# One transformer layer in split single precision: operands loaded in place, last sums moved into gate and up, last projections reordered, memory laid out anew

## The chip, the cores and the metric

One core of a Trainium2 chip runs the kernel. The metric is device microseconds from start to end, as the median of several runs. Engines are named as in the profile: PE is TensorE, DVE VectorE, ACT ScalarE, POOL GpSimd; SP is SyncE, whose queue issues nearly all DMA transfers here. Lines are written L91, and they are lines of the kernel before unless said otherwise.

## The reference

One layer over a sequence of 2048 positions of width 1024, in float32: a mixing half (band attention beside a gMLP) and a SwiGLU feed-forward half, each with a norm ahead and a residual behind.

```python
h = rmsnorm(x, mix_norm_g)
q, k, v, u, vg = split(h @ w_in)                  # 1024 -> 2560
a = band_attention(q, k, v, ...)                  # 8 heads of 64, chunks of 64, 8 chunks back
g = spatial_gating(u, vg, ...)                    # blocks of 128 positions, 8 groups
mix = concat(rmsnorm(a, att_out_norm_g), rmsnorm(g, gmlp_out_norm_g))
x = x + mix @ w_out                               # 1024 -> 1024
h = rmsnorm(x, ffn_norm_g)
gate, up = split(h @ w_ffn_in)                    # 1024 -> 2 * 2816
x = x + (silu(gate) * up) @ w_ffn_out             # 2816 -> 1024
```

## The kernel before

**Precision.** Every large product is three matmuls. `split` (L86) makes of a float32 operand a rounded part (a cast on ACT) and the rest (a subtraction on DVE); `mm3` (L90) adds high by high, high by low and low by high into one PSUM bank. A 128x512 matmul of this kind begins every 0.2267 us.

**Stages.** 1: input projection, gMLP, early attention heads, up to about 530 us. 2: the late heads (tiles 4 to 15 of 128 positions), and between their scores, `flip` and `values` pieces of the output projection, up to 916 us. 3: gate and up. 4: the down-projection. Stages 1 and 2 write PE's order by hand (`manual_schedule`); all other orders are set by a scheduler at build time, which works with a model of the machine.

**Stage 2.** `out_piece(m, n, kt)` (L584) is one `mm3` for tile m, half n of the 1024 columns and one of eight 128-row blocks; kt 0 to 3 are the gMLP half of the input (woh4 to woh7), 4 to 7 the attention half. `mix_g` and `mix_a` (L139, L142) transpose a half of the mixed input on PE and split it into mh and ml. At kt = 7, DVE adds the bank to xm, ACT squares and sums, POOL makes the factor (L81, L83), DVE writes the normalised tile h2 (L599). `operands(m)` (L603) then makes eight transposes of it on PE, copies them into hT on ACT and stores them to y_d. `add_fill` writes the list of pieces, and `feed` takes from it.

**What y_d is.** Gate and up are made with seven products of half size in place of eight (a Strassen form): of a tile t of the first four in its half of the sequence and tile t + 4 come the seven moving operands y_d[hf][o], four of which are sums, made by four 128x512 subtractions on POOL (L620 to L623) as soon as tile t + 4 is there. hf is the half of the sequence (tiles 0 to 7, 8 to 15).

**Stage 3.** For each hf and each p = 0 to 10 (256 columns of 2816) there are 14 products: o = 0 to 6, and s = 0 for gate, 1 for up. A product is 12 matmuls (`product`, L770). Weights: `w_raw` loads wir, `w_sums` makes s3, s1 (in wir) and s2 on POOL, `w_op` splits one operand into wih and wil; `generate` runs five products ahead. `prep(hf)` loads the seven moving operands into three buffers (gt3, which also hold the results g) as ynat, four DMAs of 256 KB each with pieces of 512 bytes, and splits each into yh and yl in two halves. `use` and `emit` bring the banks into g; at the end of each p, g and c go to f_d. For hf = 1 the seven operands are loaded and split again while PE goes on.

**Stage 4.** `product` (L871) runs seven products of 22 halves each: ar from f_d, split into ah and al, and a weight, split into oh and ol. The weights of the first product (w11, called w_0, w_2 ... in the order) are kept, the first two in the pool wk40.

**Memory.** Pools are laid out by hand at the left or right end of the memory, and a tile that lies where another was waits for the last reader or writer of that one. Before the change the first wih buffers and the weight sums (wi3, sum3) share addresses with mx2, that holds hT and the sums t of the last tile; wk40 and part of wt4 in stage 4 share with gt3.

## Time and profile before

| | |
|---|---|
| median of 3 runs | 2232.69 us (2232.06 to 2233.97) |
| profiled execution | 2236.06 us |
| its span, first to last instruction | 2234.3 us |
| mean granted clock of PE | 0.988 |
| PE busy | 2160.9 us (97%), 12090 matmuls |
| DVE busy | 1295.2 us (58%) |
| ACT busy | 901.9 us (40%) |
| POOL busy | 920.1 us (41%) |
| DMA | 356.60 MB, mean 160 GB/s |

A profile of one execution gives for each engine its instructions with start and length, and for idle time what released the engine at its end. PE's time in the span is nearly all busy, so what is left to win is in a few gaps; they are found in the list of waits and then read in the timeline of the place. A busy time of one matmul is longer than the distance between two, because they overlap.

### The profile page before, as it was taken

The numbers are of one execution on the slowest core, as the hardware profiler recorded it, in microseconds if no ns is written. First come the engines' busy times: TensorE is split into PE (matmuls) and PEld (weight loads), VectorE is DVE, ScalarE is ACT, GpSimd is POOL, SyncE is SP. The second block draws the span as 40 slices with busy tenths as digits, with TensorE's granted clock in tenths as the row PEclk, the third lists the DMA queues.
The fourth block names the chain that finished last, engine by engine and source line by source line (L and its number), as shares of the span: only waits on it lengthen the run. The fifth ranks groups of instructions, "written<-read, shape, count | busy, mean of one in ns | idle before, by whom it ended". The sixth has DMA issues, their size and how long they took to land.

```text
span 2234.3 us, 32028 instructions
## 1 busy us (share of the span) xinstructions
PE 2160.9 (97%) x12090; PEld 1797.2 (80%) x12090; DVE 1295.2 (58%) x1809; ACT 901.9 (40%) x1639; POOL 920.1 (41%) x792
## 2 busy tenths in 40 slices
PE   8999999999999999599999999999999979999999
PEld 7888887887888888478888887788888858888787
DVE  4367335774677666566565668666566524545554
ACT  6434444543555555433333334333333323222322
POOL 1253114330002101556666665767666512613444
PEclk9999999999999999799999999999999989999999
DMA  7243615648878875822322327232323343733473
GB/s 257 80 132 117 222 57 170 167 145 259 286 225 278 269 237 170 269 90 90 122 91 104 108 94 229 93 123 90 123 90 121 138 150 128 278 136 110 156 240 139
DMA packets 183802, 356.60 MB, mean 160 GB/s; under 512 B 15328, under 2 KB 68576, under 8 KB 182112
## 3 DMA queue, kind: packets, MB, share of 16 engines
q1 hardware_dynamic: 183504, 354.55, 48.1%
q8 instruction: 95, 1.56, 0.3%
q14 instruction: 59, 0.48, 0.1%
q10 hardware_dynamic: 144, 0.00, 0.0%
HBM read 253.83 MB, written 100.66 MB: 159 GB/s over the span
## 4 chain that ended last, share of the span: by engine, by line
PE 53%; DMA 2%; DVE 2%; SPq 1%; issue 1%; POOL 1%; ACT 0%; DVEq 0%; ACTq 0%; POOLq 0%
PE bank L91 18%; PE bank L93 18%; PE bank L92 18%; DMA ynat<-y_d 1%; DVE yl L88 1%; SPq L723 0%; DMA y_d<-t 0%; DVE wil L88 0%; DMA w<-in_w_fo 0%; SPq L845 0%; DMA b<-y_d 0%; POOL t L621 0%; DVE xo L894 0%; POOL wir L742 0%; DMA wir<-in_w_fi 0%
## 5 line engine op out<-in xcount | busy, mean ns | idle before, releaser
L91 PE MATMUL bank<-yh,wih 128*128 128x512 f32 x1232 | 481.6, 391 | 17.2 <-ACT wih L87 17.2
L93 PE MATMUL bank<-yh,wil 128*128 128x512 f32 x1232 | 480.9, 391 | 4.4 <-DVE wil L88 4.1
L92 PE MATMUL bank<-yl,wih 128*128 128x512 f32 x1232 | 481.0, 390 | 0.0
L91 PEld LDWEIGHTS bank<-yh,wih 128*128 128x128 f32 x1232 | 232.3, 189 | 66.1 <-ACT wih L87 18.1
L93 PEld LDWEIGHTS bank<-yh,wil 128*128 128x128 f32 x1232 | 231.9, 188 | 55.4 <-DVE wil L88 7.3
L92 PEld LDWEIGHTS bank<-yl,wih 128*128 128x128 f32 x1232 | 232.4, 189 | 48.6
L91 PE MATMUL ps<-wh,xh 128*128 128x512 f32 x640 | 252.4, 399 | 7.9 <-ACT wh L87 7.9
L91 PE MATMUL bank<-oh,ah 128*128 128x512 f32 x616 | 239.9, 392 | 15.4 <-ACT oh L87 15.4
L92 PE MATMUL ps<-wl,xh 128*128 128x512 f32 x640 | 251.4, 394 | 2.5 <-DVE wl L88 2.5
L93 PE MATMUL ps<-wh,xl 128*128 128x512 f32 x640 | 251.2, 393 | 0.0
L92 PE MATMUL bank<-ol,ah 128*128 128x512 f32 x616 | 239.6, 389 | 0.0
L88 DVE TENSOR_TENSOR al<-ar,ah 128x1024 fp32r<-128x1024 f32 x77 | 107.8, 1400 | 211.4 <-ACT ah L87 211.4
L93 PE MATMUL bank<-oh,al 128*128 128x512 f32 x616 | 220.8, 389 | 2.1 <-DVE al L88 2.1
L88 DVE TENSOR_TENSOR wil<-s,wih 128x512 fp32r<-128x512 f32 x132 | 134.0, 1017 | 122.6 <-ACT wih L87 122.6
L87 ACT CAST wih<-s 128x512 fp32r<-128x512 f32 x132 | 81.9, 622 | 303.6 <-POOL s L743 158.3
L88 DVE TENSOR_TENSOR wil<-wir,wih 128x512 fp32r<-128x512 f32 x176 | 195.4, 1111 | 6.3 <-ACT wih L87 6.3
L87 ACT CAST ah<-ar 128x1024 fp32r<-128x1024 f32 x77 | 81.2, 1055 | 284.5 <-PE bank L92 266.5
L87 ACT CAST wih<-wir 128x512 fp32r<-128x512 f32 x176 | 108.9, 621 | 188.3 <-PE bank L92 178.0
L781 POOL TENSOR_TENSOR g<-up,g 128x512 f32<-128x512 f32 x88 | 122.8, 1395 | 108.9 <-DVE up L780 80.6
L91 PEld LDWEIGHTS bank<-oh,ah 128*128 128x128 f32 x616 | 116.6, 190 | 40.3 <-ACT oh L87 15.8
L91 PEld LDWEIGHTS ps<-wh,xh 128*128 128x128 f32 x640 | 121.2, 190 | 31.2 <-ACT wh L87 7.9
L92 PEld LDWEIGHTS ps<-wl,xh 128*128 128x128 f32 x640 | 121.1, 189 | 26.7 <-DVE wl L88 3.5
(182 smaller groups left out, 4051.3 us busy)
## 6 DMA issues: line engine op xcount, KB each, us to landing
wir<-in_w_fi SPq DMA_DIRECT2D x88, 512.0 KB, 4.4
ar<-f_d SPq DMA_DIRECT2D x77, 512.0 KB, 3.3
kTw<-kT_d SPq DMA_DIRECT2D x96, 320.0 KB, 4.2
f_d<-g SPq DMA_DIRECT2D x22, 1024.0 KB, 4.0
wr<-in_w_in SPq DMA_DIRECT2D x40, 512.0 KB, 5.0
f_d<-c SPq DMA_DIRECT2D x22, 768.0 KB, 6.1
wor<-in_w_fo SPq DMA_DIRECT2D x66, 256.0 KB, 3.5
ynat<-y_d SPq DMA_DIRECT2D x56, 256.0 KB, 5.1
```

Of the source, the lines that this page charges most:

```text
L87: nc.scalar.copy(hi, src)
L88: nc.vector.tensor_sub(lo, src, hi.bitcast(F32))
L91: nc.tensor.matmul(ps, lhsT=lh, rhs=rh, start=first, stop=False)
L92: nc.tensor.matmul(ps, lhsT=lh, rhs=rl, start=False, stop=False)
L93: nc.tensor.matmul(ps, lhsT=ll, rhs=rh, start=False, stop=last)
L781: nc.gpsimd.tensor_tensor(g[:, i], t, g[:, i], op=ALU.mult)
```

## The change

Four things are changed together.

*In place.* `prep` has no buffers of its own. Each operand is loaded into the memory of its yl, as float32; ACT casts it into yh and DVE subtracts in place. There are two DMAs of 512 KB for an operand, with pieces of 4 KB, and yh and yl keep the order (tile, block k, column), so that a product's moving operand, `y[:, :, k]`, is four blocks of 128 columns. y_d is one tensor for the four tiles of an operand.

*The last tiles' sums.* For tiles 13, 14, 15 `operands` stores the two halves of hT alone. `combine(n)`, n = 0 to 5, makes the sums for 256 columns: four loads, four subtractions on POOL, four stores. They are written in the loops p = 2 to 7 of hf = 0; the scheduler puts them into p = 0 to 2.

*The last projections.* `add_tail` writes the pieces of tiles 14 and 15: tile 14's gMLP half for both n, tile 15's, `operands(13)`, tile 14's attention half, tile 15's, with `operands(14)` in it. Both banks of these tiles are one tile of pS.

*Memory.* The projection weights are four pools instead of one, and stage 3's pools lie so that wi3, sum3, wr3 and y0 are over the attention's buffers, y1 and y2 over woh4 to woh7, y3 and y4 over woh0 to woh3, y5 and y6 over mixed inputs and h2. gt3 has two buffers. wk40 and wt4 of stage 4 are now over wi3 and wr3.

The diff, cut:

```diff
-    y_d = [[[dram.tile([P, 512], F32, name=f"y_d{i}_{o}_{j}") for j in range(4)] for o in range(7)] for i in range(2)]
+    y_d = [[dram.tile([P, 4, 512], F32, name=f"y_d{i}_{o}") for o in range(7)] for i in range(2)]
+    h_d = {m: dram.tile([P, 512], F32, name=f"h_d{m}") for m in range(NT - 3, NT)}
...
-        for n, bufs in (("pr", 3), ("pp", 2), ("an", 2), ("sa", 4), ("vt", 6), ("bt", 1), ("qd", 2), ("kw", 5)):
+        for n, bufs in (("pr", 3), ("pp", 2), ("sa", 4), ("vt", 6), ("bt", 1), ("qd", 2), ("kw", 5), ("an", 2)):
...
-        wo2, mx["T"] = pool(stack, "wo2", 1), pool(stack, "mxT", 2)
         for kt in (4, 5, 6, 7, 0, 1, 2, 3):
+            if kt % 2 == 0:
+                wo2 = pool(stack, f"wo2{kt}", 1)
...
+        mx["T"] = pool(stack, "mxT", 2)
...
-        hp = pool(st_out, "h2", 1)
-        mx["2"], sm = pool(st_att, "mx2", 2, "right"), pool(st_att, "sm2", 4, "right")
+        mx["2"], hp, sm = pool(st_att, "mx2", 2, "right"), pool(st_att, "h2", 1, "right"), pool(st_att, "sm2", 4, "right")
...
-                po[m, n] = pS.tile([P, 2, 512], F32, tag="S", name="po")[:, 0] if flush and n else pO.tile([P, 512], F32, tag="po", name="po")
+                if m < NT - 2:
+                    po[m, n] = pO.tile([P, 512], F32, tag="po", name="po")
+                elif n == 0:
+                    both = pS.tile([P, 2, 512], F32, tag="S", name="po2")
+                    po[m, 0], po[m, 1] = both[:, 0], both[:, 1]
...
-            y = [y_d[hf][o][t % 4] for o in range(7)]
-            if t < 4:
+            y = [y_d[hf][o][:, t % 4] for o in range(7)]
+            if m in h_d:
+                nc.sync.dma_start(h_d[m], hT[:, :512])
+                nc.sync.dma_start(y[5], hT[:, 512:])
+            elif t < 4:
...
-            if m == NT - 1:
-                fill.extend(("piece", piece(n, kt)) for kt in range(KT) for n in range(2))
-                fill.insert(len(fill) - 4, ("operands", m - 1))
-                return
...
-                    if kt == 3 and m > 0:
+                    if kt == 3 and m > 0 and (n == 0 or m < NT - 3):
                         fill.append(("a" if n else "g", m + 1))
+
+        def add_tail():
+            def half(m, kts):
+                fill.extend(("piece", lambda n=n, kt=kt: out_piece(m, n, kt)) for n in range(2) for kt in kts)
+
+            m = NT - 1
+            half(m - 1, range(4))
+            fill.extend((("a", m - 1), ("g", m)))
+            half(m, range(4))
+            fill.append(("operands", m - 2))
+            half(m - 1, range(4, 8))
+            fill.append(("a", m))
+            half(m, range(4, 8))
+            fill.insert(len(fill) - 3, ("operands", m - 1))
...
-        for m in range(NT):
+        for m in range(NT - 2):
             add_fill(m)
...
+                if i == len(LATE):
+                    add_tail()
...
-        yp = {0: pool(st, "y0", 1, "right")}
-        gt, wr, wi, sp3 = (pool(st, n, b, "right") for n, b in (("gt3", 3), ("wr3", 1), ("wi3", 6), ("sum3", 1)))
-        for i in (1, 2):
-            yp[i] = pool(st, f"y{i}", 1)
+        y0, wr, wi, sp3, gt = (pool(st, n, b, "right") for n, b in (("y0", 1), ("wr3", 1), ("wi3", 6), ("sum3", 1), ("gt3", 2)))
+        yp = [y0] + [pool(st, f"y{i}", 1) for i in range(1, 6)]
         tm = pool(st, "tm3", 1)
-        for i in (3, 4, 5, 6):
-            yp[i] = pool(st, f"y{i}", 1, "left" if i < 5 else "right")
-        cb = pool(st, "cb3", 1, "right")
+        yp.append(pool(st, "y6", 1))
+        cb, df = pool(st, "cb3", 1), pool(st, "df3", 1)
...
-                yh = yp[o].tile([P, 4, 512], F32R, tag="yh", name=f"yh{hf}{o}")
-                yl = yp[o].tile([P, 4, 512], F32R, tag="yl", name=f"yl{hf}{o}")
+                yh = yp[o].tile([P, 4, 4, P], F32R, tag="yh", name=f"yh{hf}{o}")
+                yl = yp[o].tile([P, 4, 4, P], F32R, tag="yl", name=f"yl{hf}{o}")
                 ys.append((yh, yl))
-                r = gt.tile([P, 4, 512], F32, tag="g", name="ynat")
-                for i in range(4):
-                    nc.sync.dma_start(r[:, :, i * P : (i + 1) * P], y_d[hf][o][i].rearrange("p (k t) -> p k t", k=4))
-                for k in range(0, 4, 2):
-                    split(yh[:, k : k + 2], yl[:, k : k + 2], r[:, k : k + 2])
+                for i in (slice(0, 2), slice(2, 4)):
+                    r = yl[:, i].bitcast(F32)
+                    nc.sync.dma_start(r, y_d[hf][o][:, i].rearrange("p i (k t) -> p i k t", k=4))
+                    split(yh[:, i], yl[:, i], r)
             return ys
+
+
+        def combine(n):
+            m, c = NT - 3 + n // 2, slice(n % 2 * 256, n % 2 * 256 + 256)
+            y = [y_d[1][o][:, m % 4, c] for o in range(7)]
+            h1, h2, b1, b2, t1, t2, t3, t4 = (df.tile([P, 256], F32, tag=t, name=t) for t in ("dh1", "dh2", "db1", "db2", "dt1", "dt2", "dt3", "dt4"))
+            for dst, src in ((h1, h_d[m][:, c]), (h2, y[5]), (b1, y[0]), (b2, y[4])):
+                nc.sync.dma_start(dst, src)
+            nc.gpsimd.tensor_sub(t1, h1, b1)
+            nc.gpsimd.tensor_sub(t2, h2, t1)
+            nc.gpsimd.tensor_sub(t3, h2, h1)
+            nc.gpsimd.tensor_sub(t4, b2, t2)
+            for o, src in ((1, t2), (2, t1), (3, t3), (6, t4)):
+                nc.sync.dma_start(y[o], src)
...
+            bk = bk.rearrange("p (i t) -> p i t", i=4)
             for k in range(4):
-                mm3(bk, w[0][:, k], w[1][:, k], y[0][:, k], y[1][:, k], k == 0, k == 3)
+                mm3(bk, w[0][:, k], w[1][:, k], y[0][:, :, k], y[1][:, :, k], k == 0, k == 3)
...
+            if hf == 0 and 2 <= p < 8 and (o, s) == (1, 0):
+                combine(p - 2)
```

In the orders below, rows are instructions of one engine in sequence; the line numbers of the second fence of a pair are those of the kernel after (L92 to L94 is `mm3`, L613 the transposes of `operands`, L739 the loads of `prep`, L749 and L755 the loads and stores of `combine`, L762 `w_raw`).

PE at the end of stage 2 and the start of stage 3, before: the last piece of tile 15 (po), the transposes of tile 15 (pth), the first product (bank).

```order
L91 MATMUL po<-woh_5184,mh_11363 128x512
L92 MATMUL po<-wol_5185,mh_11363 128x512
L93 MATMUL po<-woh_5184,ml_11364 128x512
L608 MATMUL pth<-ident,h_11546 128x128 x8
L91 MATMUL bank<-yh_11678,wih 128x512
L92 MATMUL bank<-yl_11679,wih 128x512
```

After: the same last piece, then the first product (yh_11610 is operand o = 0), and in product o = 2 (yh_11626) the transposes of tile 15.

```order
L92 MATMUL po_11354<-woh_5151,mh_11345 128x512
L93 MATMUL po_11354<-wol_5152,mh_11345 128x512
L94 MATMUL po_11354<-woh_5151,ml_11346 128x512
L92 MATMUL bank<-yh_11610,wih 128x512
L93 MATMUL bank<-yl_11611,wih 128x512
L94 MATMUL bank<-yh_11610,wil 128x512
...
L94 MATMUL bank<-yh_11626,wil 128x512
L613 MATMUL pth<-ident,h_11486 128x128 x8
L92 MATMUL bank<-yh_11626,wih 128x512
```

The transposes have moved from ahead of the first gate/up matmul to behind 33 of them.

SP at the start of stage 3, before: the last stores of tile 15's sums between the last operand loads, then the weights of p = 1 and the results of p = 0.

```order
L625 DMA y_d_2_3_166<-t_11565 128x512
L723 DMA ynat<-y_d_6_2_153 128x4x128
L723 DMA ynat<-y_d_6_3_154 128x4x128
L625 DMA y_d_1_3_162<-t_11566 128x512
L625 DMA y_d_6_3_182<-t_11568 128x512
L733 DMA wir<-in_w_fi 128x1024 x4
L830 DMA f_d_183<-g 128x4x512
```

After: the weights of p = 1 between the loads and stores of the first two combines (dh and db are loads, dt stores).

```order
L762 DMA wir<-in_w_fi 128x1024
L739 DMA yl_11659<-y_d_6_133 128x1024 x2
L749 DMA dh_12301<-h_d_141 128x256
L749 DMA dh_12302<-y_d_5_139 128x256
L749 DMA db_12303<-y_d_0_134 128x256
L749 DMA db_12304<-y_d_4_138 128x256
L762 DMA wir<-in_w_fi 128x1024
L755 DMA y_d_3_137<-dt_12307 128x256
L755 DMA y_d_2_136<-dt_12305 128x256
L749 DMA dh_12617<-h_d_141 128x256
L755 DMA y_d_1_135<-dt_12306 128x256
```

The stores wait for POOL's subtractions, and the next weight loads now stand behind some of them.

SP from stage 3 to stage 4, before: the last result goes to f_d between the first weights of the down-projection, of which w_0 is used first.

```order
L875 DMA ar<-f_d_187 128x1024
L830 DMA f_d_193<-g 128x4x512
L845 DMA w_4_18461<-in_w_fo 128x512
L831 DMA f_d_193<-c 128x3x512
L845 DMA w_6_18497<-in_w_fo 128x512
...
L845 DMA w_16_18677<-in_w_fo 128x512
L845 DMA w_0_18389<-in_w_fo 128x512
```

After: eleven of these weights, w_0 first, and then the last result.

```order
L907 DMA ar<-f_d_148 128x1024
L877 DMA w_0_18400<-in_w_fo 128x512
L877 DMA w_2_18436<-in_w_fo 128x512
...
L877 DMA w_20_18760<-in_w_fo 128x512
L862 DMA f_d_154<-g 128x4x512
```

w_0 has moved ahead of the store that waits for stage 3's last result.

## Rows read from the trace of the kernel before

**Rows 1.** PE's waits: line, releaser: us in total, times, longest

```profile
PE bank L91 <- ACT wih L87: 17.2, 2, 15.6
PE bank L91 <- ACT oh L87: 15.4, 1, 15.4
...
PE pth L608 <- DVE h L599: 7.6, 1, 7.6
```

**Rows 2.** Timeline, PE, 890 to 954: start, length, instruction [idle before <-releaser]

```profile
890.90 0.50 PE L91 MATMUL po<-woh,mh 128*128 128x512 f32 x1 [0.78 <-DVE xm L591]
...
915.82 0.39 PE L93 MATMUL po<-woh,ml 128*128 128x512 f32 x1
923.78 1.94 PE L608 MATMUL pth<-ident,h 128*128 128x128 f32 x8 [7.57 <-DVE h L599]
941.35 0.80 PE L91 MATMUL bank<-yh,wih 128*128 128x512 f32 x1 [15.63 <-ACT wih L87]
...
953.70 0.63 PE L93 MATMUL bank<-yh,wil 128*128 128x512 f32 x1
```

**Rows 3.** Timeline, POOL and ACT, 936 to 943

```profile
937.20 1.26 POOL L741 TENSOR_TENSOR s<-wir 128x512 f32<-128x512 f32 x1 [3.29 <-DMA y_d<-t]
...
940.68 1.14 ACT L87 CAST wih<-wir 128x512 fp32r<-128x512 f32 x2 [8.69 <-DMA y_d<-t]
941.73 1.99 ACT L87 CAST yh<-ynat 128x1024 fp32r<-128x1024 f32 x2
```

**Rows 4.** Timeline, DVE: gate evacuation of product 6, p = 1, 2, 9; last p = 9

```profile
1021.66 0.69 DVE L776 TENSOR_TENSOR g<-bank,u 128x512 f32<-128x512 f32 x1 [1.96 <-PE bank L93]
...
1059.74 0.69 DVE L776 TENSOR_TENSOR g<-bank,u 128x512 f32<-128x512 f32 x1 [1.96 <-PE bank L93]
...
1326.30 0.69 DVE L776 TENSOR_TENSOR g<-bank,u 128x512 f32<-128x512 f32 x1 [1.96 <-PE bank L93]
...
1750.94 0.69 DVE L776 TENSOR_TENSOR g<-bank,u 128x512 f32<-128x512 f32 x1 [1.96 <-PE bank L93]
```

**Rows 5.** Timeline, DVE, 1332 to 1391: subtractions of split

```profile
1332.28 1.78 DVE L88 TENSOR_TENSOR wil<-s,wih 128x512 fp32r<-128x512 f32 x1
...
1343.05 0.69 DVE L88 TENSOR_TENSOR wil<-s,wih 128x512 fp32r<-128x512 f32 x1 [1.86 <-ACT wih L87]
...
1361.28 2.31 DVE L88 TENSOR_TENSOR yl<-ynat,yh 128x1024 fp32r<-128x1024 f32 x1
...
1388.68 2.36 DVE L88 TENSOR_TENSOR yl<-ynat,yh 128x1024 fp32r<-128x1024 f32 x2 [1.11 <-ACT yh L87]
```

**Rows 6.** Timeline, PE, 1791 to 1811

```profile
1791.31 0.39 PE L93 MATMUL bank<-yh,wil 128*128 128x512 f32 x1
1807.12 3.56 PE L91 MATMUL bank<-oh,ah 128*128 128x512 f32 x8 [15.43 <-ACT oh L87]
```

**Rows 7.** Timeline, SP's queue and ACT, 1769 to 1808

```profile
1769.97 9.82 SPq L875 DMA_DIRECT2D ar<-f_d  x5
1793.93 0.37 SPq L830 DMA_DIRECT2D f_d<-g  x1
...
1806.45 1.76 ACT L87 CAST oh<-w 128x512 fp32r<-128x512 f32 x3 [16.08 <-DMA w<-in_w_fo]
```

**Rows 8.** Timeline, PE, spatial gating (vh in blocks) and attention: matmuls of 256 columns

```profile
89.02 0.28 PE L92 MATMUL pm<-vl,wsh 128*128 128x256 f32 x1
...
89.97 0.28 PE L91 MATMUL pm<-vh,wsh 128*128 128x256 f32 x1
...
397.18 0.40 PE L186 MATMUL Ss<-ke,qe 128*128 128x256 f32 x2
```

**Rows 9.** Part 6 of the page: DMA issues, KB each, median us to landing

```profile
wir<-in_w_fi SPq DMA_DIRECT2D x88, 512.0 KB, 4.4
...
wor<-in_w_fo SPq DMA_DIRECT2D x66, 256.0 KB, 3.5
...
ynat<-y_d SPq DMA_DIRECT2D x56, 256.0 KB, 5.1
```

More of the change, by code (lines that the diff above doesn't have):

```diff
@@ L574, in block_kernel @@
                 load_tile(NE + 1)
+        pV = pool(st, "pV", 1, space=PSUM)
+        pO = pool(st, "pO", 1, space=PSUM)
         pS = pool(st, "pS", 2, space=PSUM)
         pT = pool(st, "pT", 2, space=PSUM)
-        pV = pool(st, "pV", 1, space=PSUM)
         mx["P"] = (pT, "pt")
-        pO = pool(st, "pO", 1, space=PSUM)
         po = {}
-        flush = False
         def out_piece(m, n, kt):
@@ L695, in block_kernel @@
                         att_norm(m)
-            flush = True
             while fill:
```

## The prediction

> **What bounds the kernel now.** Read the busy times first: TensorE (PE) works 2160.9 of the 2234.3 us span, 97%, at a mean granted clock of 0.988 (both in the table above). The change takes away no matmul, so it can only win idle time and time at the low clock, 73.4 us plus what the clock costs. The list of PE's waits tells where that is [rows 1]: one wait of 15.6 us for the first gate/up weight, one of 15.4 us for the first down-projection weight, one of 7.6 us for the last normalised tile. Everything else named there is 5 us or less. So three places decide, and I call them A (stage 2 to 3), M (where gate and up change from the first eight sequence tiles to the last eight, at about 1360 to 1420 us) and B (stage 3 to 4).
>
> At A the timeline of PE shows what stands between the last projection matmul and a stage 3 at speed [rows 2]: the last piece begins at 915.82, then 7.57 us of waiting for h of tile 15, its eight transposes, 15.63 us for the first weight, and then matmuls at the low clock (0.63 us for one at 953.70 where the same line takes 0.39 at full clock, as at 915.82). The other engines say why [rows 3]: the sums that make the first weights begin on GpSimd (POOL) only at 937.20, and the first weight cast on ACT at 940.68, both released by a store of y_d out of a tile t. They don't compute with t. Their memory is what t and hT held (first wih buffers and weight sums share addresses with mx2), so the wait is one for memory, that of tile 15.
>
> How much A costs altogether is read from a mark in the loop: the gate evacuation of product 6. It comes once in every loop of p. Between those of p = 2 and p = 9 lie seven undisturbed loops [rows 4]: (1326.30 - 1059.74) / 7 = 38.08 us each. That is 14 products of 2.72, or 168 matmuls of 0.2267. The mark of p = 1 is at 1021.66.
>
> **Part by part: A.** The change lays first weights and sums over kw, qd, bt, vt, which are free when attention ends; makes tile 15's four 512-column subtractions a matter of stage 3; and orders the last pieces so that h of tile 13 and 14 have pieces to hide behind. Tile 15's eight transposes now stand three quarters through product 2 of stage 3, 33 matmuls or 7.5 us after the last piece. Working: the last piece ends for PE at 915.82 + 0.23 = 916.05. Without the wait of 0.78 in front of tile 15's first pieces [rows 2], which goes since both halves of a late tile own two banks, that is 915.3. From there 1.0 us for the transposes, 27 products of 2.72 = 73.4 to the mark of p = 1, and 0.2 from matmul to mark: 989.9, against 1021.66. With no stall A gives **31.8**.
>
> I don't take all of it, since the added waits stand in the same 25 us. VectorE (DVE) and ACT execute in order, and their rows now mix three things: mh/ml of the last tiles, the seven loaded operands' splits, the weights' splits. Each yl half is a subtraction of 1.18 us alone (2.36 for two) [rows 5]. (1) The gMLP half of tile 15 comes right behind its transposes, with no other pieces between: one yl half (1.2) and the 0.7 of ml stand before it: estimate 2. (2) ml of tile 15's attention half stands on DVE behind three halves whose memory (y1, y2 over woh4 to woh7) is free only when the gMLP halves are through: 48 matmuls and two groups of transposes from 890.9, with the 2 of (1) about 904. A load of 5.1 us [rows 9], a cast of 1.0 [rows 3], subtractions of 1.2, 0.7 and 0.7 and a us for issue and hand-overs follow: ml at about 913, where PE is through with the 24 matmuls and 12 transposes between at 911. Estimate 3, with h of tile 13 in it. (3) h of tile 15 took 7.6 us more than no work in between; now 7.5 us of products cover it, with a fuller DVE: estimate 1. (4) The combines: 24 loads, 24 subtractions of 256 columns and 24 stores. SP has them between the wir loads of p = 1 and p = 2, POOL between those weights' sums, and an SP store waits for its subtraction with the next wir load queued behind it. A weight sum of p = 1 is by my chain ready about 2 us before PE wants it, in p = 2 about 3. I take 1 for it. Sum for A: 31.8 - 7 = **25**, bounds 12 (rival 1) and 32.
>
> **M.** In the 424.64 us between the marks at 1326.30 and 1750.94 there are 11 loops of 38.08 = 418.88, so M loses 5.8 now [rows 4]. There DVE is the busiest but PE, with the yl subtractions at 2.31 in place of 1.18 beside POOL [rows 5]. In place, a load cannot begin before PE's last read of that yl, where before three spare buffers took it early; but the seven loads are then spread over the first loop as PE lets go, with 4 KB runs instead of 512 bytes (28 loads of 512 KB for 56 of 256 KB; a 512 KB load took 4.4 us, a 256 KB one of the old form 5.1) [rows 9]. From PE's last read of one o to its next there are 14 products less two, 32 us, against 5 for the load and 2 x (1.05 + 2.3) for splits: it fits if nothing queues. Estimate **3**, bounds 5.8 and -4 (three operands late, each by what load 4.4, cast 1.0, subtraction 2.3 and a us of hand-overs overrun two products of 2.72, 3.3 us, so 10 lost where 5.8 are now).
>
> **B.** PE's last stage-3 matmul begins at 1791.31, the first of stage 4 at 1807.12, and its first eight take 3.56 instead of 1.81 [rows 6]: 15.6 + 1.75 = 17.3 lost. The reason is on SP [rows 7]: five ar loads done at 1779.8, then nothing until f_d<-g at 1793.93, which waits for the last products' result, and the w loads behind it (w_0 eighth of them), so that oh was cast at 1806.45. Their memory (wk40, wt4) was that of the g tiles. After the change w_0 is the first load behind the ar loads, and its memory is that of early-released weights. It is issued about 1780, lands by 1785 (256 KB took 3.5 to 5.1 [rows 9]), and the cast must only wait for ACT's last silu: the second-last product ends 2.72 before 1791.5, its evacuation of 0.7 and the silu follow, about 1790.4. PE begins with eight products oh x ah, 1.8 us, in which ol is made. Estimate 0.5 left: **16.8**. Bounds: 17.3, and 10 if the cast is still behind the last results (DVE and POOL's at 1791 to 1794, load and split 6).
>
> **At no cost.** The moving operand of the 3696 gate/up matmuls becomes four blocks of 128 columns, 2 KB apart. The trace has such a form in the spatial gating, where vh is read in blocks of 64: one begins every 0.119 us (89.02 to 89.97, eight) [rows 8], and a plain one of 256 columns takes 0.12 (two in 0.40, one 0.28). So nothing. The subtraction in place reads and writes what it did, at the same addresses.
>
> **Sum.** 25 + 3 + 16.8 = 44.8. The profiled execution's 2236.06 becomes 2191.3; it lies 1.8 above its span and 3.4 above the median of the runs, so **2188** for 2232.69. All best 2178, all worst (12, -4, 10) 2215.
>
> **Rivals.** *1, DVE and POOL hold each other up in the tail.* POOL used to be in its t sums then; now it makes the eight first weight sums (1.26 each) beside the fourteen yl halves. A split beside POOL took 2.31 for 1.18, the small one 1.78 for 0.69 [rows 5]. If all are hit, 14 x 1.1 = 15.4 us more of DVE before the first products, of which PE gets most: A falls to 12, M to 0: 2232.69 - 12 - 16.8 = 2204. For it: M shows just this mixture. Against it: the weight sums are done early, once, 10 us in all. The Trainium skill, "SBUF — State Buffer", section "SBUF: two separate sides", says that a DVE operation with two SBUF inputs and a GpSimd operation take a shared port pair by an exclusive lock for a whole instruction; the rows at 0.69 and 1.78 agree with that, and by it every split that meets a sum would wait its full time, which is this rival. Chance 0.18.
>
> *2, the combines block SP.* Each is a chain of load, subtraction and store, some 10 us, with wir of p = 1 and 2 queued among them. If two stand in front of a wir load, PE waits about 10 in each of two loops: 2188 + 20 = 2208. For it: SP issues in order and the six were put into three loops. Against: tiles have one buffer, but the wir loads stand between, not behind all. 0.07.
>
> *3, slower: the strided moving operand costs.* If a block's start costs PE time, it does so 3696 times: the gain of 44.8 is gone from 12.1 ns for each (5% of 226.7). At 30 ns: +111 - 45, about 2299. For it: the precedent has shorter blocks and half the columns. Against: its pace is exactly that of the plain form. 0.03.
>
> *4, the first weights don't come early.* If their memory (kw, qd, bt) waits for a last reader or its loads queue behind y stores, A stays and B alone comes: 2232.69 - 16.8 - 3 = 2213. Against: SP has the four first wir loads ahead of tile 12's y_d stores. 0.05.
>
> **How the numbers follow.** Forecast 0.67, its own range 2178 to 2200. With rivals 1 and 2 in, 2178 to 2208; outside are rivals 3 and 4 and what the forecast and rival 2 leave at the ends, about 0.15 to 0.2. 0.2% is 4.5 us, about what a measurement here can tell from no change. All but rival 3 and a mishap I don't see are faster: 0.94; same 0.02, slower 0.04.
>
> **What would show it.** A right: mark of p = 1 near 997, PE's wait list without the two entries of 15.6 and 7.6, PE gap under 1 at the stage's start, no clock below 0.9 from 900 to 1000. Rival 1: yl rows of 2.3 and PE waits "yl" or "ml" of over 3 before 930. Rival 2: PE waits for wih in p = 1 and 2 with DMA wir behind it. Rival 3: loop not 38.08. B right: oh's wait under 2. M: 11 loops between the marks plus 3. Wrong altogether if loads into yl delay each other so that products of p = 0 wait one by one, or if the reordering leaves PE idle long enough in the tail for the clock to fall.

## The result, and the profile after

The kernel after takes 2204.65 us (2204.1 to 2205.32, four runs) for 2232.93 before: ratio 0.9873, 95% interval 0.9856 to 0.989. That is 28.3 us faster, and 17 us slower than the 2188 forecast. It lies outside the forecast's own range (2178 to 2200) and inside the one that takes in rivals 1 and 2 (2178 to 2208), near its upper end.

The page of the kernel after begins so; the second block's rows have one digit for each fortieth of the span:

```profile
span 2202.7 us, 32056 instructions
...
PE 2158.4 (98%) x12090; PEld 1795.7 (82%) x12090; DVE 1301.0 (59%) x1809; ACT 900.6 (41%) x1639; POOL 928.1 (42%) x804
...
PEclk9999999999999999999999999999999999999999
```

PE's idle time in the span falls from 73.4 to 44.3 us, and no slice shows a granted clock below 0.9 any more; stretches of some us at the low clock are still there, as will be seen. The list of PE's waits of the kernel after (line, releaser: total, times, longest), to be held against [rows 1]:

```profile
PE po L92 <- DVE xm L596: 6.6, 6, 3.7
PE bank L94 <- DVE wil L89: 4.9, 3, 3.4
...
PE bank L92 <- ACT wih L88: 3.9, 3, 2.3
```

The waits of 15.6, 15.4 and 7.6 us are gone. In their place stand smaller ones: for xm of the last tiles, for wih and wil, and, in the timeline below, for mh and ml.

To see which place won what, I cut each profiled execution at three points: the last wait of PE for a bank of tile 13 in stage 2 (0.28 us, at 880.64 before and 880.23 after), the gate mark of p = 9 in the first half, and the same mark in the second half. The marks of the kernel after, DVE's timeline, answering [rows 4]:

```profile
1043.08 0.69 DVE L806 TENSOR_TENSOR g<-bank,u 128x512 f32<-128x512 f32 x1 [1.28 <-PE bank L94]
...
1309.64 0.69 DVE L806 TENSOR_TENSOR g<-bank,u 128x512 f32<-128x512 f32 x1 [1.96 <-PE bank L94]
...
1736.37 0.69 DVE L806 TENSOR_TENSOR g<-bank,u 128x512 f32<-128x512 f32 x1 [1.96 <-PE bank L94]
```

The first two are those of p = 2 and p = 9: (1309.64 - 1043.08) / 7 = 38.08 us a loop, exactly as before. All kernels of this study, us of their profiled executions; each ratio is to runs of the kernel before taken beside that kernel, with medians from 2232.93 to 2235.3:

| kernel | A: to the mark of p = 9 | M: to that of the second half | B: to the end | median, ratio to before |
|---|---|---|---|---|
| before | 445.66 | 424.64 | 483.4 | 2232.93 |
| after | 429.41 | 426.73 | 466.3 | 2204.65, 0.9873 (0.9856 to 0.989) |
| after_again | 428.23 | 427.83 | 468.0 | 2202.49, 0.9855 (0.9842 to 0.9868) |
| b_weights_first | 442.59 | 423.78 | 466.1 | 2217.55, 0.992 (0.9906 to 0.9933) |
| b_inplace | 443.33 | 426.95 | 487.2 | 2238.03, 1.0015 (1.0005 to 1.0024) |
| two_tiles | 429.19 | 427.18 | 467.4 | 2204.89, 0.9857 (0.984 to 0.9875) |
| old_order | 425.62 | 426.82 | 467.2 | 2201.19, 0.9848 (0.983 to 0.9866) |
| late_sums | 428.00 | 427.39 | 467.1 | 2204.56, 0.9861 (0.9844 to 0.9878) |
| tail_sums | 428.92 | 427.26 | 467.3 | 2204.22, 0.9865 (0.9851 to 0.988) |
| old_tail | 424.04 | 426.57 | 466.2 | 2199.85, 0.9852 (0.9832 to 0.9872) |
| old_late2 | 424.41 | 426.49 | 468.8 | 2200.05, 0.9847 (0.9833 to 0.9862) |
| hf1_no_sub | 429.42 | 418.88 | 467.9 | 2197.99, 0.9831 (0.9816 to 0.9846) |
| best1 | 446.79 | 427.18 | 469.5 | 2223.63, 0.9947 (0.9933 to 0.9961) |
| best2 | 427.76 | 427.73 | 470.5 | 2205.42, 0.9864 (0.9848 to 0.9881) |

Before to after: A gives 16.3 (25 forecast), M costs 2.1 (a gain of 3 forecast), B gives 17.0 (16.8 forecast). With 0.4 ahead of A that is the 31.6 us between the spans; the medians are 28.3 apart because the profiled execution of before lies 3.1 above the median here and that of after at its own. Each part is from one profile a kernel: before and b_weights_first have the same code as far as the mark of p = 9, and their A differs by 3.1; after and its repeat differ by 1.2.

**B.** PE's timeline where stage 4 begins, and SP's queue ahead of it, in the kernel after, against [rows 6, 7]:

```profile
1776.75 0.39 PE L94 MATMUL bank<-yh,wil 128*128 128x512 f32 x1
1776.97 1.98 PE L92 MATMUL bank<-oh,ah 128*128 128x512 f32 x8
```

```profile
1765.74 6.85 SPq L877 DMA_DIRECT2D w<-in_w_fo  x11
1779.70 0.38 SPq L862 DMA_DIRECT2D f_d<-g  x1
```

The first matmul of stage 4 begins 0.22 us after the last one of stage 3, at full clock: nothing of the 17.3 us is left. The eleven weights are issued from 1765.74 on, 14 us ahead of the store that held them up before.

**A.** PE's timeline at the end of stage 2, kernel after, against [rows 2]:

```profile
896.87 0.50 PE L92 MATMUL po<-woh,mh 128*128 128x512 f32 x1 [1.74 <-ACT mh L88]
...
898.83 0.50 PE L94 MATMUL po<-woh,ml 128*128 128x512 f32 x1 [1.23 <-DVE ml L89]
...
911.46 0.79 PE L92 MATMUL po<-woh,mh 128*128 128x512 f32 x1 [3.68 <-DVE xm L596]
912.05 0.63 PE L93 MATMUL po<-wol,mh 128*128 128x512 f32 x1
...
918.43 0.50 PE L92 MATMUL po<-woh,mh 128*128 128x512 f32 x1 [0.67 <-ACT mh L88]
...
922.50 0.50 PE L92 MATMUL po<-woh,mh 128*128 128x512 f32 x1 [0.79 <-DVE xm L596]
```

896.87 is tile 15's gMLP half waiting for its split, 2.97 us in both rows. 911.46 is tile 14's attention half n = 1, and it waits 3.68 us until DVE has taken the finished half n = 0 out of its bank; after that, 12 matmuls and four transposes run at the low clock (0.43 us from one matmul to the next at 912.05, 0.2267 at full; granted clock 0.66 from 910 to 920), 2.8 us more. 922.50 is the same wait for tile 15. DVE's timeline there shows why its evacuation came so late:

```profile
907.32 2.35 DVE L89 TENSOR_TENSOR wil<-wir,wih 128x512 fp32r<-128x512 f32 x2
909.60 1.21 DVE L89 TENSOR_TENSOR yl<-yl,yh 128x1024 fp32r<-128x1024 f32 x1
910.73 0.68 DVE L596 TENSOR_TENSOR xm<-po,xm 128x512 f32<-128x512 f32 x1
```

Two weight splits and an operand split of stage 3 stand ahead of it in DVE's queue. In p = 1 POOL's timeline has the sums of combine (dt, three in a row here) ahead of the weight sums (s), and PE waits for the weight made from the sum of 972.31:

```profile
967.73 0.75 POOL L753 TENSOR_TENSOR dt<-db,dt 128x256 f32<-128x256 f32 x1
968.43 0.73 POOL L750 TENSOR_TENSOR dt<-dh,db 128x256 f32<-128x256 f32 x1
969.13 0.73 POOL L752 TENSOR_TENSOR dt<-dh,dh 128x256 f32<-128x256 f32 x1
...
972.31 1.30 POOL L772 TENSOR_TENSOR s<-wir 128x512 f32<-128x512 f32 x1
```

```profile
974.31 0.50 PE L92 MATMUL bank<-yh,wih 128*128 128x512 f32 x1 [0.71 <-ACT wih L88]
...
976.13 0.51 PE L94 MATMUL bank<-yh,wil 128*128 128x512 f32 x1 [1.08 <-DVE wil L89]
```

With the like pair in p = 2 (0.81 and 0.40) that is 3.0 us of waits.

**M.** PE, DVE and ACT where the second half of the sequence begins, kernel after:

```profile
1360.90 0.50 PE L92 MATMUL bank<-yh,wih 128*128 128x512 f32 x1 [2.34 <-ACT wih L88]
...
1365.23 0.79 PE L94 MATMUL bank<-yh,wil 128*128 128x512 f32 x1 [3.43 <-DVE wil L89]
```

```profile
1359.59 3.91 DVE L89 TENSOR_TENSOR yl<-yl,yh 128x1024 fp32r<-128x1024 f32 x2
...
1364.02 1.16 DVE L89 TENSOR_TENSOR wil<-s,wih 128x512 fp32r<-128x512 f32 x1
```

```profile
1359.70 0.63 ACT L807 ACTIVATE g<-g 128x512 f32<-128x512 f32 x1 [2.54 <-DVE g L806]
1360.23 0.61 ACT L88 CAST wih<-s 128x512 fp32r<-128x512 f32 x1
```

DVE runs without a gap. The weight split that PE waits for at 1365.23 begins at 1364.02, behind two operand subtractions that took 3.91 us instead of 2.4; the cast on ACT was held up in the same way, by a silu that waited for DVE. The two waits are 5.8 us, and the low clock behind them (granted clock 0.66 from 1360 to 1370) brings M's loss against eleven loops of 38.08 to 7.9.

The loads in place are not late. The first subtraction for yl of the second half, kernel before and kernel after:

```profile
1354.11 4.35 DVE L88 TENSOR_TENSOR yl<-ynat,yh 128x1024 fp32r<-128x1024 f32 x2
```

```profile
1327.98 1.22 DVE L89 TENSOR_TENSOR yl<-yl,yh 128x1024 fp32r<-128x1024 f32 x1 [4.05 <-ACT yh L88]
```

From the mark of p = 9 (1326.30 and 1309.64) that is 27.8 us before and 18.3 after.

### The profile page after: what moved, and what is told of

It is laid out like the page before. It is cut to its first block, busy times and chain, and to the rows that moved or that the text cites. A ratio compares the mean times of both kernels' runs of the same rounds, so it can differ in the third digit from the quotient of the medians.

```text
span 2202.7 us, 32056 instructions
## 1 busy us (share of the span) xinstructions
PE 2158.4 (98%) x12090; PEld 1795.7 (82%) x12090; DVE 1301.0 (59%) x1809; ACT 900.6 (41%) x1639; POOL 928.1 (42%) x804
## 4 chain that ended last, share of the span: by engine, by line
PE 78%; issue 9%; DMA 5%; POOL 4%; DVE 3%; ACT 1%; SPq 0%; DVEq 0%; POOLq 0%; ACTq 0%
PE bank L94 17%; PE bank L92 17%; PE bank L93 17%; PE ps L92 6%; PE ps L93 6%; PE ps L94 6%; PE S L182 1%; PE pt L209 1%; PE po L94 1%; PE po L92 1%; PE po L93 1%; PE pv L221 1%; DMA yl<-y_d 1%; DMA be<-in_bias 1%; DVE yl L89 1%
## 5 line engine op out<-in xcount | busy, mean ns | idle before, releaser
L94 PE MATMUL bank<-yh,wil 128*128 128x512 f32 x1232 | 480.4, 390 | 4.9 <-DVE wil L89 4.9
L92 PE MATMUL bank<-yh,wih 128*128 128x512 f32 x1232 | 480.3, 390 | 3.9 <-ACT wih L88 3.9
L94 PEld LDWEIGHTS bank<-yh,wil 128*128 128x128 f32 x1232 | 231.6, 188 | 54.6 <-DVE wil L89 6.4
L92 PEld LDWEIGHTS bank<-yh,wih 128*128 128x128 f32 x1232 | 231.6, 188 | 52.9 <-ACT wih L88 5.1
L92 PE MATMUL ps<-wh,xh 128*128 128x512 f32 x640 | 252.4, 399 | 7.8 <-ACT wh L88 7.8
L94 PE MATMUL ps<-wh,xl 128*128 128x512 f32 x640 | 251.8, 394 | 0.0
L92 PE MATMUL bank<-oh,ah 128*128 128x512 f32 x616 | 238.4, 389 | 0.0
L94 PE MATMUL bank<-oh,al 128*128 128x512 f32 x616 | 220.8, 389 | 2.1 <-DVE al L89 2.1
L89 DVE TENSOR_TENSOR wil<-s,wih 128x512 fp32r<-128x512 f32 x132 | 140.8, 1069 | 117.6 <-ACT wih L88 117.4
L92 PEld LDWEIGHTS ps<-wh,xh 128*128 128x128 f32 x640 | 121.2, 190 | 31.1 <-ACT wh L88 7.8
L94 PEld LDWEIGHTS ps<-wh,xl 128*128 128x128 f32 x640 | 121.0, 189 | 25.2
```

What stands on the lines that cost most here:

```text
L89: nc.vector.tensor_sub(lo, src, hi.bitcast(F32))
L92: nc.tensor.matmul(ps, lhsT=lh, rhs=rh, start=first, stop=False)
L94: nc.tensor.matmul(ps, lhsT=ll, rhs=rh, start=False, stop=last)
```

## The experiments

**b_weights_first** changes only the layout of stage 4 in the kernel before.

```diff
-        xo, t4, wk0, wt, ca, cb = (
-            pool(st, n, b, "right") for n, b in (("xo4", 8), ("tm4", 4), ("wk40", 1), ("wt4", 3), ("ca4", 1), ("cb4", 1)))
+        wk0, wt, xo, t4, ca, cb = (
+            pool(st, n, b, "right") for n, b in (("wk40", 1), ("wt4", 3), ("xo4", 8), ("tm4", 4), ("ca4", 1), ("cb4", 1)))
```

> The kernel before, with one thing changed: in stage 4 the pools of the first weights (wk40, wt4) are laid ahead of xo4 and tm4, so they lie over y0 and not over gt3. Theory: the 15.6 us of waiting and 1.75 us of low clock at the start of stage 4 are memory alone: the first weight is loaded while stage 3 still runs, the gap goes and 16 to 17 us are won, ratio 0.9925 to 0.993 to the kernel before. Rival: the loads stay behind the store of the last result on SP, or what now lies over gt3 (xo, tm) is late instead: less than 8 us, ratio over 0.9965.

Measured: 2217.55 us, ratio 0.992 (0.9906 to 0.9933), and part B goes from 483.4 to 466.1. PE's wait of 15.4 us for oh is gone. The gain of B is memory alone: the first weights lay over buffers that were free only after the last result, and a layout that puts them elsewhere gives all of it.

**b_inplace** is the kernel before with the operands loaded in place.

```diff
...
-                r = gt.tile([P, 4, 512], F32, tag="g", name="ynat")
-                for i in range(4):
-                    nc.sync.dma_start(r[:, :, i * P : (i + 1) * P], y_d[hf][o][i].rearrange("p (k t) -> p k t", k=4))
...
+                for i in (slice(0, 2), slice(2, 4)):
+                    r = yl[:, i].bitcast(F32)
+                    nc.sync.dma_start(r, y_d[hf][o][:, i].rearrange("p i (k t) -> p i k t", k=4))
...
-                mm3(bk, w[0][:, k], w[1][:, k], y[0][:, k], y[1][:, k], k == 0, k == 3)
+                mm3(bk, w[0][:, k], w[1][:, k], y[0][:, :, k], y[1][:, :, k], k == 0, k == 3)
```

> The kernel before with the loads in place alone (prep, y_d's shape and the products' moving operand as in the kernel after; memory, order and last sums as before). Theory: at the change of halves DVE is the bound either way; loads in place begin later, so the loss of 5.8 us becomes 7.5 to 8.5, and at the start of stage 3 nothing is won since the first weights still wait for tile 15's sums: 1 to 3 us slower than before, ratio 1.000 to 1.0015; the loop stays 38.08. Rival: the smaller number of DMAs (28 for 56) on SP and the free third buffer help both places: 3 to 8 us faster, ratio 0.9965 to 0.9987.

Measured: 2238.03 us, ratio 1.0015 (1.0005 to 1.0024): 3.7 us slower by the medians. M costs 2.3 us more than before, with the two waits that the kernel after has:

```profile
1372.77 0.50 PE L91 MATMUL bank<-yh,wih 128*128 128x512 f32 x1 [2.03 <-ACT wih L87]
...
1377.09 0.79 PE L93 MATMUL bank<-yh,wil 128*128 128x512 f32 x1 [3.59 <-DVE wil L88]
```

A is 2.3 better in its one profile, which is no more than two runs of one order differ here (445.66 and 442.59, for before and b_weights_first), and the wait for the first weight is still there:

```profile
936.61 0.79 PE L91 MATMUL bank<-yh,wih 128*128 128x512 f32 x1 [15.52 <-ACT wih L87]
```

B is 3.8 longer in that profile, with the same waits (15.5 for oh, 2.05 for al) and more time at the low clock behind them (granted clock 0.66 from 2117 to 2122, where before has 1.00 at the same place, from 2118 to 2123). So of the 3.7 us only M's 2.3 are put down to the loads. They are no gain in themselves; that their place in the change is to give up a buffer of gt3 and so make room for the layout was argued and not tried. The loop stays 38.08 with the strided operand.

**hf1_no_sub** leaves out the 14 subtractions for yl in the second half of the sequence, in the kernel after.

```diff
-                    split(yh[:, i], yl[:, i], r)
+                    if hf == 0:
+                        split(yh[:, i], yl[:, i], r)
+                    else:
+                        nc.scalar.copy(yh[:, i], r)
```

> The kernel after, but for the second half of the sequence the 14 subtractions on DVE that make yl are left out (yl stays the loaded operand, so the output is not the reference's). At the change of halves the kernel after loses 7.9 us against 38.08 us a loop. Theory: DVE is the bound there, with 14 subtractions of 1.2 to 2.3 us in some 40 us, and casts, evacuations and weights queue behind them: the loss falls to under 1.5, 2197 to 2199. Rival: the loads in place come too late, since they wait for PE's last read of yl: the loss stays above 5, 2202 to 2205.

Measured: M is 418.88 us, eleven times 38.08 to the hundredth, and the time falls to 2197.99. The marks:

```profile
1307.92 0.69 DVE L809 TENSOR_TENSOR g<-bank,u 128x512 f32<-128x512 f32 x1 [1.96 <-PE bank L94]
...
1726.80 0.69 DVE L809 TENSOR_TENSOR g<-bank,u 128x512 f32<-128x512 f32 x1 [1.96 <-PE bank L94]
```

All 7.9 us of M hang on DVE's subtractions; the loads in place, which still wait for PE's last read, cost nothing by themselves.

**two_tiles** gives the four accumulators of tiles 14 and 15 a PSUM tile each.

```diff
-                elif n == 0:
-                    both = pS.tile([P, 2, 512], F32, tag="S", name="po2")
-                    po[m, 0], po[m, 1] = both[:, 0], both[:, 1]
+                elif m == NT - 2:
+                    po[m, n] = pS.tile([P, 2, 512], F32, tag="S", name="po")[:, 0]
+                else:
+                    po[m, n] = (pO if n == 0 else pV).tile([P, 512], F32, tag="pv" if n else "po", name="po")
```

> The kernel after, with the four accumulators of tiles 14 and 15 in four PSUM tiles of their own (two of pS, pO, pV) in place of two two-bank tiles. Theory: in the kernel after PE waits 3.68 us and 0.79 us for DVE's evacuation of half n = 0 before it may go on with half n = 1, because both halves are one tile; the 3.68 also brings 2.8 us of low clock. Then both waits and the low clock go, and what is late next is mh and ml of tile 15's attention half on ACT and DVE (ACT waits there for an operand load): of 7.3 us between 2 and 7 come back, 2198 to 2203. Rival: the releaser is named wrongly and PE waits for DVE's place in its queue whatever the tiles are: the wait of 3.7 stays, 2204 to 2205.

Measured: 2204.89 us, ratio 0.9857 (0.984 to 0.9875), and A 429.19 where after and its repeat have 429.41 and 428.23: no gain. The time is the rival's, but not by its cause: the wait of 3.68 is gone, so it came from the shared tile: the build orders accesses by tile, and two banks of one tile are not independent in it. What came in its place is the next wait that the theory named, on PE and ACT:

```profile
911.19 0.60 PE L134 MATMUL ptm<-ident,a 128*128 128x128 f32 x4
915.20 0.50 PE L92 MATMUL po<-woh,mh 128*128 128x512 f32 x1 [3.42 <-ACT mh L88]
...
917.11 0.80 PE L94 MATMUL po<-woh,ml 128*128 128x512 f32 x1 [1.08 <-DVE ml L89]
```

```profile
912.42 1.04 ACT L88 CAST yh<-yl 128x1024 fp32r<-128x1024 f32 x1 [2.22 <-DMA yl<-y_d]
913.62 1.04 ACT L88 CAST yh<-yl 128x1024 fp32r<-128x1024 f32 x1 [0.16 <-DMA yl<-y_d]
914.57 0.58 ACT L88 CAST mh<-ptm 128x512 fp32r<-128x512 f32 x1
```

The transposed half of tile 15 is ready at 911.8, but ACT has casts of two operand halves ahead of it, and the first of them waits for a DMA. 4.5 us take the place of 4.5, and the low clock came behind this wait too (granted clock 0.90, 0.78 and 0.87 in the three stretches of 10 us from 900 to 930, for 1.00, 0.66 and 1.00 in the kernel after).

**old_order** is the kernel after with the last projections in the order of before, and their PSUM tiles (pO, and pS for the second halves at the end).

```diff
...
-        for m in range(NT - 2):
+        for m in range(NT):
             add_fill(m)
...
-                if i == len(LATE):
-                    add_tail()
...
+            if m == NT - 1:
+                fill.extend(("piece", piece(n, kt)) for kt in range(KT) for n in range(2))
+                fill.insert(len(fill) - 4, ("operands", m - 1))
+                return
```

> The kernel after with the order of the last projections of before (tile 14's halves n one after the other, tile 15's n interleaved) and its PSUM tiles. Theory: the gain at the start of stage 3 comes from the memory of the first weights, not from the order; without the order the wait of 3.7 and its low clock are not there, the wait before tile 15 (0.8) and the gap for h of tile 14 come back: between 2200 and 2208. Rival: the order is what hides h of tiles 13 and 14 and the split of tile 15, and without it 5 us and more are lost with another clock fall: 2209 to 2216.

Measured: 2201.19 us, ratio 0.9848 (0.983 to 0.9866); A is 425.62, 2.6 to 3.8 less than in the two profiles of the kernel after. PE's waits in stage 2, and a matmul behind the last of them:

```profile
892.91 0.50 PE L92 MATMUL po<-woh,mh 128*128 128x512 f32 x1 [2.15 <-DVE xm L593]
...
903.24 0.63 PE L610 MATMUL pth<-ident,h 128*128 128x128 f32 x4 [0.19 <-DVE h L601]
905.96 1.07 PE L610 MATMUL pth<-ident,h 128*128 128x128 f32 x4 [2.09 <-DVE ml L89]
...
907.25 0.63 PE L93 MATMUL po<-wol,mh 128*128 128x512 f32 x1
```

That is 4.4 us in three waits. The clock falls here too (granted clock 0.83 from 900 to 910): four transposes and six matmuls behind the last wait run at the low level, some 1.7 us more. The kernel after has 8.1 us in five waits and 2.8 of low clock. The new order is no part of the gain.

**late_sums** puts the buffers of combine into that of c, so that the scheduler cannot draw them together.

```diff
...
-            h1, h2, b1, b2, t1, t2, t3, t4 = (df.tile([P, 256], F32, tag=t, name=t) for t in ("dh1", "dh2", "db1", "db2", "dt1", "dt2", "dt3", "dt4"))
+            d = cb.tile([P, 4, 512], F32, name="d", tag="c")
+            h1, h2, b1, b2, t1, t2, t3, t4 = (d[:, j // 2, j % 2 * 256 : j % 2 * 256 + 256] for j in range(8))
...
```

> The kernel after, with the loads and sums of combine in the buffer of c (bufs 1), so that each combine has to wait for the stores of one p and stands in a loop of its own, p = 2 to 7. Theory: the waits of 0.71, 1.08, 0.81 and 0.40 us in p = 1 and 2 come from POOL making 256-column sums between the weight sums; spread out they go: 3 us faster, 2201 to 2202. Rival: the weights of p = 1 and 2 are late because wir loads stand on SP behind combine's stores, and each loop then pays once, six times instead of twice: 2206 to 2215.

Measured: 2204.56 us, ratio 0.9861 (0.9844 to 0.9878). The waits of p = 1 and 2 are gone, but between the marks of p = 2 (1038.08) and p = 9 (1306.94) lie 268.86 us instead of 266.56: 2.3 of the 3.0 us come back a little at a time in the loops that now hold a combine. Both theories had their part, and the sum is near nothing.

**tail_sums** and **old_tail** make the last tiles' sums at once in stage 2, as before, the second with the old order too.

```diff
-            if m in h_d:
-                nc.sync.dma_start(h_d[m], hT[:, :512])
-                nc.sync.dma_start(y[5], hT[:, 512:])
-            elif t < 4:
+            if t < 4:
...
-            if hf == 0 and 2 <= p < 8 and (o, s) == (1, 0):
-                combine(p - 2)
```

> The kernel after with the sums of the last three tiles made at once in stage 2, as before, and no combine; order and memory as after. Theory: combine costs the four waits of p = 1 and 2, 3 us; without it they go, and the twelve 512-column subtractions on POOL in the tail lie in memory that nothing early needs; they lengthen some of DVE's subtractions there. From the anchor in stage 2 to the mark of p = 9: 425 to 429 us where the kernel after has 428.2 to 429.4; ratio 0.984 to 0.9865. Rival: moving these sums out is what makes the gain at the start of stage 3; with them back the first weights or the first operands wait for POOL and the tail again: 433 us and more, ratio over 0.988.

> The same with the order of the last projections of before too: what is left of the change is the loads in place and the memory. Theory: memory alone makes the gain at the start of stage 3, and order and combine cost 3.8 and 3: from anchor to the mark of p = 9 421 to 426 us (445.7 before, 425.6 with the old order and combine); ratio 0.983 to 0.985. Rival: order or moved sums are needed as well: over 430, ratio over 0.987.

Measured: A is 428.92 and 424.04. So combine costs 0.5 us in the new order (429.41 - 428.92; against the repeat it would be a gain of 0.7) and 1.6 in the old one, less than its four waits, because without it others come: in tail_sums PE waits 0.74 and 1.54 us for yh and yl in p = 0 instead. And the old order is better by 4.9 here, as by 3.8 in the pair with combine. What remains in old_tail, loads in place and memory, has more than the whole gain at A: 21.6 us (18.5 against b_weights_first's A) where the full change has 16.3. As the loads alone left the wait of 15.5 us where it was (b_inplace), it is the layout that takes it away. Whether late sums and the new order would have taken it away without the layout was not tried.

**old_late2** joins the old order and combine in the buffer of c (with three of the differences written over their inputs, so that the buffer keeps its size).

```diff
...
+            d = cb.tile([P, 3, 512], F32, name="d", tag="c")
+            h1, h2, b1, b2, t2 = (d[:, j // 2, j % 2 * 256 : j % 2 * 256 + 256] for j in range(5))
+            t1, t3, t4 = b1, h1, b2
...
```

> The kernel after with the order of the last projections of before, and combine's sums in the buffer of c, one in each of the loops p = 2 to 7. Theory: the order gives 3.8 us and the spread sums 1 to 2 (3 less in p = 1 and 2, 1 to 2.3 more in later loops): from anchor to the mark of p = 9 423 to 425 us, ratio 0.983 to 0.985. Rival: with the tail shorter, the sums meet the weights of p = 1 all the same: 426 or more, as with the old order alone.

Measured: A 424.41, 2200.05 us, ratio 0.9847 (0.9833 to 0.9862), as expected; a third pair, 3.6 us better than late_sums, its nearest kernel with the new order.

**best1** is old_late2 with the second half's operands split ahead, in the loops of the first half, and stored as yh and yl.

```diff
...
+        def early_split(o, j):
+            i = slice(2 * j, 2 * j + 2)
+            h, l = (df.tile([P, 2, 512], F32R, tag=f"e{n}", name=f"e{n}") for n in "hl")
+            nc.sync.dma_start(l.bitcast(F32), y_d[1][o][:, i])
+            split(h, l, l.bitcast(F32))
+            nc.sync.dma_start(yh_d[o][:, i], h.bitcast(F32))
+            nc.sync.dma_start(yl_d[o][:, i], l.bitcast(F32))
...
+                    if hf:
+                        for t, d in ((yh, yh_d), (yl, yl_d)):
+                            nc.sync.dma_start(t[:, i].bitcast(F32), d[o][:, i].rearrange("p i (k t) -> p i k t", k=4))
+                        continue
```

> The kernel after with three changes: the order of the last projections of before; the last sums in the buffer of c, one combine in a loop; and the seven operands of the second half split early, in loops p = 2 to 9 of the first half (14 loads, casts, subtractions and two stores each), so that at the change of halves yh and yl are only loaded. Theory: 3.8 us from the order, 1.4 to 3 from the sums, and 6 to 7.9 at the change of halves, where without the 14 subtractions nothing was lost: 10 to 14 us below the kernel after, ratio to the kernel before 0.9805 to 0.983. Rival: the early splits collide with the weights of the first loops (SP stores behind them, DVE beside POOL) and lose there 1 us in each of ten loops: about as the kernel after, 0.986 to 0.988.

Measured: 2223.63 us, worse than the rival had it. Between 1000 and 1300 us PE's list has 18 waits for weights where the kernel after has two. SP's list of the same stretch has, in the queue that also issues the weight loads (L766), stores of early splits (L740) that wait for their cast and stores of combine (L759) that wait for their subtraction:

```profile
PE bank L93 <- ACT wih L89: 11.2, 9, 1.7
PE bank L95 <- DVE wil L90: 6.1, 9, 1.7
```

```profile
SPq L740 <- ACT eh L89: 32.4, 8, 5.2
...
SPq L759 <- POOL d L754: 14.8, 6, 5.1
```

That SP's queue is what makes the weights late was read from these lists, and not tried by itself.

And M is no better (427.18): twice the bytes have to come in there, and one wait of 2.1 us is now for the DMA of yh. Of the 7.9 us nothing was won this way.

**best2** was to take away the wait of 2.15 us of old_late2; its difference to old_late2 is this.

```diff
-                po[m, n] = pS.tile([P, 2, 512], F32, tag="S", name="po")[:, 0] if flush and n else pO.tile([P, 512], F32, tag="po", name="po")
+                po[m, n] = pS.tile([P, 2, 512], F32, tag="S", name="po")[:, 0] if flush and m == NT - 1 else pO.tile([P, 512], F32, tag="po", name="po")
```

> The kernel after with the order of the last projections of before, the sums of the last tiles one in a loop in the buffer of c, and both accumulators of tile 15 in PSUM tiles of pS, so that its first piece doesn't wait until DVE has emptied the bank of tile 14. Theory: the wait of 2.15 us in front of tile 15's first pieces goes and of it 1 to 2 us reach the mark of p = 9: anchor to mark 422 to 423.5 us (424.4 with the bank shared), ratio 0.982 to 0.9845. Rival: tile 15's split is then late by the same amount, as with the two tiles in the new order: 424 to 425, ratio 0.984 to 0.986.

Measured: A 427.76, 2205.42 us, worse than theory and rival had it. The wait stayed and a second one came, with the low clock behind it (granted clock 0.74 from 897 to 910, for 1.00 in old_late2):

```profile
889.89 0.50 PE L92 MATMUL po<-woh,mh 128*128 128x512 f32 x1 [2.15 <-DVE xm L593]
...
897.98 0.50 PE L92 MATMUL po<-woh,mh 128*128 128x512 f32 x1 [1.86 <-DVE xm L593]
```

I had the tile wrong: counted by pieces, the first is tile 14's first half waiting for tile 13's bank, and the edit took from tile 14's second half the bank that spared it a wait. The 0.78 of [rows 2] is that same place, not tile 15 as the prediction says.

**after_again** is the kernel after once more.

> The kernel after once more, for comparison on the same chip. Theory: the waits are set by the orders of the engines and come again: 1.7 and 1.2 us before tile 15's first pieces, 3 to 4.5 between tile 14's halves, 3 us in p = 1 and 2, 5 to 6 at the change of halves; ratio 0.986 to 0.988. Rival: they move about with the DMA and each execution has others: the marks at p = 9 differ by more than 3 us against the same anchor in stage 2.

Measured: ratio 0.9855 (0.9842 to 0.9868). The waits are at the same places, with 2.24 us instead of 3.68 between tile 14's halves, less than the 3 to 4.5 expected. tail_sums (2.06) and hf1_no_sub (2.22) also have some 2 us there, and late_sums 4.28. Between tile 15's halves, where nothing stands in DVE's queue, the same wait is 0.78 or 0.79 in after and its repeat; what is longer than that in the kernel after is DVE's queue.

Old_order, old_tail and old_late2 (2199.85 to 2201.19) beat the kernel before clearly. Against the kernel after, their ratios overlap with its two; a gain of 2.6 to 4.9 us in A is seen in every pair of profiles, but profiles of one code differ by up to 3.1 there, and its size in the median is not settled.

## Why the prediction was right or wrong, step by step

- **What bounds the kernel** was read rightly: three places, and two of them are memory. The cause at A (first weights over the last tile's sums) stands: with memory and loads in place alone, 21.6 of the 31.8 us are won, and with the loads alone the wait stays.
- **B** was forecast at 16.8 and gave 17.0; the layout alone gave 17.3. Its step that the first eight matmuls cover the split of ol holds: PE goes from stage to stage in 0.22 us and on to ol without a wait.
- **A** was mis-sized: 16.3 for 25. Against 989.9 + 38.08 = 1028.0 for the mark of p = 2 without stalls, it came at 1043.08: 15.1 lost where I allowed 7. (1) Tile 15's gMLP half was put at 2 and took 2.97. (4) The combines were put at 1, and PE waited 3.0 for them, though the kernel without them (tail_sums) is only 0.5 better at A. (3) h of tile 15 cost nothing. The step that failed is the clause on the two banks: that a wait goes "since both halves of a late tile own two banks". The wait of 0.78 went, but its place was taken by 3.68 and 0.79 between the halves of one tile, with 2.8 of low clock, 7.3 in all, for which the sum had no term. The prediction had named a fall of the clock in the tail as a sign of being wrong, and it came (0.66 from 910 to 920). (2) The wait for tile 15's attention half, put at 3 for ml, was 0.67, for mh, but only because PE came there late; where two_tiles let it come in time, mh and ml took 4.5. These terms make 13.9 of the 15.1. So the reordered tail loses these microseconds one way or the other, and the old order, which I never costed as an alternative, loses less.
- **M** was forecast as a gain of 3 and became a loss of 2.1. The step that failed: "it fits if nothing queues". The loads did fit, and the splits even begin 9.5 us earlier in the loop than with three buffers (18.3 and 27.8 us after the mark); the queue is DVE's. It is busy without a gap from 1340 to 1380, where the like stretch before, 1350 to 1390, has 37.3 of 40 us, and the weights' splits stand in it. b_inplace has nearly the same loss (8.1), so it comes with the loads in place; why the earlier splits cost 2 us more than the later ones is not shown. The bound of -4 held by luck: it was built on loads that come too late, and they did not.
- **Rival 1** gives nearly the measured time (2204), but by luck and from another sum: it had A at 12 from yl subtractions at 2.3 us and M at 0. In the tail of the kernel after, eleven of the 14 yl halves take 1.2. Its mechanism is at work in M, though. There four of the 14 subtractions take the 2.31 us of [rows 5], six take 1.2 and the rest lie between; the kernel loses 7.9 us to these subtractions. What the Trainium skill, "SBUF — State Buffer", section "SBUF: two separate sides", says of the lock agrees with the two lengths. How much of the 7.9 is the lock and how much the bare work was not separated.
- **Rival 2** held in small: 3.0 us in p = 1 and 2, by POOL more than by SP. In best1, with 42 more transfers in SP's queue and 14 more splits on ACT and DVE, A cost 22 more (446.79 for 424.41 in old_late2). **Rival 3** fell: the loop is 38.08 with the strided operand. **Rival 4** fell: the wait of 15.6 us for the first weight is gone.

## What to carry to other kernels

Where a wait is for an address and not for a value, the layout can remove it: that was 39 us here (17.3 by the layout alone, 21.6 by the layout and the loads in place that go with it), and the parts of the change that moved work (order, late sums) took some 4 to 5 of it back. Before moving work out of a gap, list for each in-order queue what will stand ahead of the evacuation that frees the next bank, and give halves that are to run one behind the other tiles of their own. When a stall goes, cost the order left as it is beside the new one.

## What the runs showed of the hardware

The clock's fall after a short wait is not the same each time. In stage 4 PE waits 2.05 us for al in every run; in the kernel after the matmuls go on at full clock, in its repeat they go on at the low one of the two levels (1.2 GHz by their distance of 0.43 us) for about eight matmuls (granted clock 1.00 and 0.57 from 2086 to 2090):

```profile
2086.15 1.42 PE L94 MATMUL bank<-oh,al 128*128 128x512 f32 x5 [2.06 <-DVE al L89]
```

```profile
2085.94 2.42 PE L94 MATMUL bank<-oh,al 128*128 128x512 f32 x5 [2.05 <-DVE al L89]
2088.16 0.63 PE L92 MATMUL bank<-oh,ah 128*128 128x512 f32 x1
```

So a wait of 2 us can cost 2 or nearly 4 us. That accounts for nearly all of the 1.7 us by which the two profiles of this kernel differ in part B (466.3 and 468.0).
